# Issuing the modulation's row tiles from GpSimd instead of SyncE in a six-stage transformer stack

## Chip, cores and metric

The kernel runs on one core of one Trainium2 chip. The metric is the device time of one execution in microseconds (us). The core's five engines have one instruction stream each: TensorE (PE, matrix products; its weight loads are shown as PEld), VectorE (DVE), ScalarE (ACT), GpSimd (POOL) and SyncE (SP). An engine works through its stream in order, and an instruction that waits holds back what stands behind it on the same engine. Transfers are issued by an engine's stream and carried out by 16 DMA engines that all issuers share.

## The reference

Four mixer layers (windowed attention, latent attention, mLSTM, windowed attention) act on 256 latent tokens and 256 context tokens of width 1024; then come a stage with three attention branches and a convolutional feed-forward stage, on the latents alone. What the change touches is the modulation of the four layers: for each layer a vector `c` (and another for the context) goes through a SiLU and a 1024 x 3072 matrix, and the three thirds of the result shift, scale and gate the layer.

```python
def modulation(cvec, w_ada, b_ada):
    return jnp.split(jax.nn.silu(cvec) @ w_ada + b_ada, 3, axis=-1)
...
        sh_l, sc_l, gt_l = modulation(c, w_ada, b_ada)
        sh_c, sc_c, gt_c = modulation(c_ctx, w_ada, b_ada)
        h_l = rmsnorm(x_lat, g_pre) * (1.0 + sc_l[:, None, :]) + sh_l[:, None, :]
        h_c = rmsnorm(x_ctx, g_pre) * (1.0 + sc_c) + sh_c
        y_l, y_c = mixer(h_l, h_c, need_ctx=need_ctx)
        x_lat = x_lat + gt_l[:, None, :] * rmsnorm(y_l, g_post)
```

## The kernel before

Activations stay in SBUF, weights are streamed from HBM once. A weight block is cut into parts of 128 x 1024 float32, 512 KB each. `load_part` (line 351) transfers such a part into one of three raw buffers `wr` (`raw`, line 374, issued on SP; from the feed-forward stage on into `wrd`), has ACT round it to a high half `wh` (line 362) and DVE compute the low half `wl` (line 364). A product of two such numbers is three matrix products: lines 384 to 386 (`gemm_a`) or 396 to 399 (`gemm_b`). `turn` (lines 636 to 646) transposes a normalised tile on PE and applies the scale and shift. The PSUM bank tag `tp` has three buffers, shared by all transposes, by `ada_first` and by the row products below.

The modulation of layer 0's shift and scale is made at the start, in four groups (`ada_first`, line 500): four blocks of 512 KB per group go into the buffers `P4` and `Q4` (line 507, on SP) and into products of line 512. Everything else of the modulation is spread over the layers as filler: `ada_steps` (line 530) is a generator that `run` (line 2061) sets up per layer, with block 2 of this layer (the gate) and blocks 0 and 1 of the next layer (scale and shift). A block is eight row tiles `ar` of 128 x 1024 float32, taken in pairs (`NADA = 2`); the pool tag `ar` has two buffers. One step of the generator first traces the product of the pair that was loaded a step before (`ada_product`, line 547, with the matmuls of line 558) and then the two transfers of the next pair. So a pair's transfers wait until the product before has read the two buffers. Layers 0, 1 and 2 have 24 row tiles each, layer 3 has 8: 80 in all. `earn` (line 401) advances the generator whenever enough matmul columns have been traced, and `drain` runs what is left at the end of a layer. `ada_gate` (line 571) and `ada_columns` (line 587) take the finished block out of PSUM; the first needs eight small transfers `br` and writes the gate to DRAM.

Every transfer of the kernel is issued on SP: `dma` (line 411), `bcast` (line 415) and `raw` (line 374). GpSimd has memsets (lines 459, 462, 1026, 1027, 1233, 1393, 1697, 1758, 1880), the scaling of line 1405 in the mLSTM layer, where DVE's line 1406 uses its result and PE transposes it (line 763), and two operations of the GELU (lines 1611 and 1612), in the three-branch stage and the feed-forward stage.

The order of instructions on each engine is not the program's: the framework plans it at build time, with priority to what is earlier in the program among the instructions whose inputs and buffers are free at that point of the plan. On the chip the streams then run in that fixed order, synchronised by semaphores.

The lines of the filler that carry the order:

```python
self.filler = self.ada_steps([(mod, 2)] + ([(nxt, 0), (nxt, 1)] if nxt is not None else []))
self.pace, self.credit = PACE[l], 0
next(self.filler)
```

Of the kernel before, what the change touches and what calls it, by code (L numbers as in the profile page):

```python
# [267 lines left out]
class Net:  # L268
# [258 lines left out]
    def ada_steps(self, blocks):  # L527

        nc, A = self.nc, self.A
        todo = None
        for mod, b in blocks:
            l = mod["l"]
            parts = WEIGHTS[f"l{l}_ada"].off[0 if l == 0 else b]
            src = A[f"w_l{l}_ada"]
            for i in range(0, len(parts), NADA):
                if todo is not None:
                    self.ada_product(*todo)
                rows = []  # L540
                for off, k, kc, n in parts[i:i + NADA]:
                    r = self.far.tile([128, 1024], F32, name=self.nm("ar"), tag="ar", bufs=NADA)
                    self.dma(r, bass.AP(tensor=src.tensor, offset=src.offset + off, ap=[[n, 128], [1, n]]))
                    rows.insert(0, (k, r))
                todo = (mod, b, rows)
                yield True
        self.ada_product(*todo)
        yield True
# [1560 lines left out]
```

## Time and profile before

| quantity | value |
|---|---|
| median of 3 runs | 1439.38 us (1436.44 to 1439.48) |
| the profiled execution | 1436.94 us |
| its span, first to last instruction | 1435.1 us |
| PE busy | 1407.4 us (98%) |
| DVE busy | 1033.9 us (72%) |
| ACT busy | 735.0 us (51%) |
| POOL busy | 47.9 us (3%) |
| moved by DMA | 203.30 MB, mean 142 GB/s |
| mean granted TensorE clock | 0.998 |

Busy time is the time in which an engine has an instruction running; issuing a transfer is not counted as busy. A matmul's end is modelled, so a busy PE is not a PE at its peak. A wait in the views below is idle time of an engine, put down to what ended it. The chain that ended last is followed back from the last instruction, at each step to what released it.

### The profile page before, as it was taken

What the parts mean: (1) busy time and instruction counts of PE and PEld (TensorE: products, weight loads), DVE (VectorE), ACT (ScalarE), POOL (GpSimd) and SP (SyncE); (2) the same over time, 40 slices, a digit from 0 to 9 for tenths busy, and PEclk for the clock granted to TensorE, in tenths of its full rate; (3) what the DMA queues carried; (4) which work ended last, traced back from release to release, by engine and by line L of the source; (5) the groups of instructions that cost most, each with busy time, mean ns of one, the idle gap of its engine ahead of it and who ended that gap; (6) DMA issues with size and microseconds to landing.
All of it is one profiled execution on the core that took longest, in us unless ns stands there. A gap on an engine that the chain in (4) does not pass through costs nothing.

```text
span 1435.1 us, 23818 instructions
## 1 busy us (share of the span) xinstructions
PE 1407.4 (98%) x9083; PEld 1149.1 (80%) x9083; DVE 1033.9 (72%) x2251; ACT 735.0 (51%) x1447; POOL 47.9 (3%) x68
## 2 busy tenths in 40 slices
PE   6999999999999999999999999999999999999998
PEld 4776667788788777777778776768978899899987
DVE  4587885653788576794766768889787887788873
ACT  3455553442466344553634555566575645565552
POOL 0000000000000000010100000000000000022210
PEclk9999999999999999999999999999999999999999
DMA  9541225345521215514252352157424444555563
GB/s 376 207 170 45 74 68 172 122 140 193 177 72 45 88 32 168 206 50 167 92 206 74 116 185 66 61 175 247 165 89 148 162 132 134 194 199 174 170 204 102
DMA packets 63553, 203.30 MB, mean 142 GB/s; under 512 B 10329, under 2 KB 14543, under 8 KB 63439
## 3 DMA queue, kind: packets, MB, share of 16 engines
q1 hardware_dynamic: 63438, 201.79, 41.7%
q8 instruction: 71, 1.16, 0.3%
q14 instruction: 44, 0.35, 0.1%
HBM read 200.65 MB, written 1.11 MB: 141 GB/s over the span
## 4 chain that ended last, share of the span: by engine, by line
PE 85%; DVE 7%; ACT 3%; DMA 3%; issue 2%; POOL 0%; SPq 0%; ACTq 0%; DVEq 0%; POOLq 0%
PE mm L384 11%; PE mm L386 11%; PE mm L385 11%; PE mm L396 8%; PE mm L399 8%; PE mm L397 8%; PE tp L989 3%; PE tp L984 3%; PE tp L558 3%; PE tp L763 2%; PE S L950 2%; PE S L399 1%; PE S L397 1%; PE S L396 1%; PE S L951 1%
## 5 line engine op out<-in xcount | busy, mean ns | idle before, releaser
L364 DVE TENSOR_TENSOR wl<-wr,wh 128x1024 fp32r<-128x1024 f32 (+5 forms) x172 | 202.0, 1181 | 56.0 <-ACT wh L362 54.1
L396 PE MATMUL mm<-th,wh 128*128 128x256 f32 (+1 forms) x712 | 220.4, 310 | 0.6 <-DVE th L771 0.6
L384 PE MATMUL mm<-wh,th 128*128 128x512 f32 (+4 forms) x544 | 215.2, 396 | 4.2 <-DVE th L645 2.1
L399 PE MATMUL mm<-th,wl 128*128 128x256 f32 (+1 forms) x712 | 217.9, 307 | 0.0
L362 ACT ACTIVATE wh<-wr 128x1024 fp32r<-128x1024 f32 (+5 forms) x172 | 175.1, 1027 | 83.3 <-PE mm L397 27.5
L386 PE MATMUL mm<-wh,tl 128*128 128x512 f32 (+4 forms) x552 | 215.4, 391 | 0.1
L397 PE MATMUL mm<-tl,wh 128*128 128x256 f32 (+1 forms) x696 | 213.4, 307 | 0.0
L385 PE MATMUL mm<-wl,th 128*128 128x512 f32 (+4 forms) x544 | 213.0, 392 | 0.0
L396 PEld LDWEIGHTS mm<-th,wh 128*128 128x128 f32 x712 | 135.7, 191 | 10.4 <-issue 4.4
L399 PEld LDWEIGHTS mm<-th,wl 128*128 128x128 f32 x712 | 135.5, 191 | 5.5 <-issue 1.1
L397 PEld LDWEIGHTS mm<-tl,wh 128*128 128x128 f32 x696 | 132.8, 191 | 5.3 <-issue 1.6
L384 PEld LDWEIGHTS mm<-wh,th 128*128 128x128 f32 x544 | 103.1, 190 | 25.6 <-issue 2.8
L386 PEld LDWEIGHTS mm<-wh,tl 128*128 128x128 f32 x552 | 104.4, 189 | 21.4 <-issue 2.2
L385 PEld LDWEIGHTS mm<-wl,th 128*128 128x128 f32 x544 | 103.1, 190 | 18.0 <-issue 0.8
L963 ACT ACTIVATE P<-S,nm 128x512 f32<-128x512 f32 (+1 forms) x96 | 58.5, 613 | 50.7 <-DVE nm L956 42.0
L364 DVE TENSOR_TENSOR wl<-wrd,wh 128x1024 fp32r<-128x1024 f32 x52 | 64.2, 1239 | 22.8 <-ACT wh L362 22.7
L385 PE MATMUL mm<-P,th 128*128 128x512 f32 x176 | 70.7, 402 | 0.0
L362 ACT ACTIVATE wh<-wrd 128x1024 fp32r<-128x1024 f32 x52 | 53.5, 1050 | 22.0 <-PE mm L385 15.7
L955 DVE TENSOR_REDUCE mx<-S 128x1 f32<-128x512 f32 (+1 forms) x80 | 54.0, 685 | 11.4 <-PE S L954 9.3
L384 PE MATMUL mm<-Q,th 128*128 128x512 f32 x144 | 57.5, 400 | 0.0
L386 PE MATMUL mm<-Q,tl 128*128 128x512 f32 x144 | 57.5, 399 | 0.0
L984 PE MATMUL tp<-eye,P 128*128 128x128 f32 x320 | 56.5, 281 | 0.0
(530 smaller groups left out, 3093.4 us busy)
## 6 DMA issues: line engine op xcount, KB each, us to landing
ar<-in_w_l_ada_dram SPq DMA_DIRECT2D x80, 512.0 KB
wr<-in_w_l_in_dram SPq DMA_DIRECT2D x48, 512.0 KB
wr<-in_w_l_out_dram SPq DMA_DIRECT2D x32, 512.0 KB
wr<-in_w_s_mg_dram SPq DMA_DIRECT2D x24, 512.0 KB
wrd<-in_w_s_down_dram SPq DMA_DIRECT2D x22, 512.0 KB
wrd<-in_w_s_gate_dram SPq DMA_DIRECT2D x20, 512.0 KB
wrd<-in_w_s_up_dram SPq DMA_DIRECT2D x20, 512.0 KB
wr<-in_w_s_br_dram SPq DMA_DIRECT2D x12, 512.0 KB
```

Source lines behind the costliest of these rows:

```text
L362: nc.scalar.activation(hi[:, :kc * n], raw[:, :kc * n], AF.Copy)
L364: nc.vector.tensor_sub(lo[:, :kc * n], raw[:, :kc * n], hi[:, :kc * n].bitcast(F32))
L384: nc.tensor.matmul(ps, xh(kk), wh[:, k, n0:n0 + n], start=kk == 0, stop=False)
L385: nc.tensor.matmul(ps, xh(kk), wl[:, k, n0:n0 + n], start=False, stop=False)
L386: nc.tensor.matmul(ps, xl(kk), wh[:, k, n0:n0 + n], start=False, stop=kk == KC - 1)
L396: nc.tensor.matmul(ps, wh[:, k, n0:n0 + m], xh(kk), start=kk == 0, stop=False)
L397: nc.tensor.matmul(ps, wh[:, k, n0:n0 + m], xl(kk), start=False, stop=False)
L399: nc.tensor.matmul(ps, wl[:, k, n0:n0 + m], xh(kk), start=False, stop=kk == KC - 1)
L558: return self.nc.tensor.matmul(ps[32 * g:32 * g + 32, :], self.cs[:, k, :], r[:, g * 256:(g + 1) * 256], start=k0 == 0 and i == 0, stop=k0 ...
L955: nc.vector.reduce_max(mx[:, r0:r0 + per], ps, axis=AX)
L963: nc.scalar.activation(p[:, :nk], ps[:, i, :], AF.Exp, scale=scale, bias=nm[:, r:r + 1], accum_out=sm[:, r:r + 1])
L984: nc.tensor.transpose(tp[:, r, :], P[r][:, j * 128:(j + 1) * 128], self.eye)
```

## The change

The two transfers of a step's row tiles are issued from GpSimd's stream instead of SP's. Source, destination, sizes, buffers and program order are the same, and all other transfers stay on SP.

```diff
@@ -540,7 +540,8 @@
                 rows = []
                 for off, k, kc, n in parts[i:i + NADA]:
                     r = self.far.tile([128, 1024], F32, name=self.nm("ar"), tag="ar", bufs=NADA)
-                    self.dma(r, bass.AP(tensor=src.tensor, offset=src.offset + off, ap=[[n, 128], [1, n]]))
+                    self.nc.gpsimd.dma_start(r, bass.AP(tensor=src.tensor, offset=src.offset + off,
+                                                        ap=[[n, 128], [1, n]]))
                     rows.insert(0, (k, r))
                 todo = (mod, b, rows)
                 yield True
```

## Rows read from the trace of the kernel before

**Rows 1.** The page: busy time by engine, shares of the chain, transfers of `ar`.

```profile
PE 1407.4 (98%) x9083; PEld 1149.1 (80%) x9083; DVE 1033.9 (72%) x2251; ACT 735.0 (51%) x1447; POOL 47.9 (3%) x68
...
PE 85%; DVE 7%; ACT 3%; DMA 3%; issue 2%; POOL 0%; SPq 0%; ACTq 0%; DVEq 0%; POOLq 0%
...
ar<-in_w_l_ada_dram SPq DMA_DIRECT2D x80, 512.0 KB
```

**Rows 2.** Windows of 25 us: length, busy by engine, granted clock, DMA share, GB/s.

```profile
0.00:25.00 25.00, 13.46 (x152) 8.98 (x153) 10.60 (x38) 9.00 (x17) 0.71 (x10) 0.93 0.94 364
...
sum 1425.00, PE 1401.10 PEld 1144.19 DVE 1032.55 ACT 734.97 POOL 47.87; mean PE 24.58 PEld 20.07 DVE 18.11 ACT 12.89 POOL 0.84
```

**Rows 3.** PE's waits, 25 to 1420 us: us in total, times, longest.

```profile
PE mm L384 <- ACT th L835: 1.6, 1, 1.6
PE tp L763 <- DVE P L1406: 1.5, 4, 0.7
...
PE tp L558 <- DMA ar<-in_w_l_ada_dram: 0.7, 1, 0.7
```

**Rows 4.** Windows of 2 us at the start, columns as in rows 2.

```profile
6.00:8.00 2.00, 0.00 (x0) 0.00 (x0) 1.18 (x7) 0.79 (x2) 0.00 (x0) 1.00 1.05 361
...
14.00:16.00 2.00, 0.46 (x5) 0.22 (x3) 1.94 (x8) 2.00 (x4) 0.00 (x0) 1.00 1.04 418
...
24.00:26.00 2.00, 2.00 (x26) 1.39 (x25) 0.55 (x5) 1.05 (x2) 0.00 (x0) 1.00 1.02 397
```

**Rows 5.** The chain that ended last, 0 to 60 us: start us, us, what.

```profile
5.30 6.89 DMA Q<-in_w_l_mod_dram
12.23 1.11 PE tp L512 x16
...
20.96 0.57 PE tp L512 x14
...
49.56 1.00 PE tp L558 x16
```

**Rows 6.** Instructions of the tile `ar`: durations min/median/max, first and last start.

```profile
L411 SPq DMA_DIRECT2D ar<-in_w_l_ada_dram x80: 327/366/1286, 30.5 to 849.9; - x80
```

**Rows 7.** SP's waits over the span: us in total, times, longest.

```profile
SPq L374 <- DVE wl L364: 588.1, 176, 19.6
SPq L411 <- PE tp L558: 176.0, 38, 26.0
```

**Rows 8.** The chain, 440 to 510 us.

```profile
470.84 4.32 DMA wr<-in_w_l_v_dram
```

**Rows 9.** The chain, 212 to 250 us.

```profile
216.08 1.04 PE tp L558 x16
...
218.09 5.54 DMA ar<-in_w_l_ada_dram
...
236.91 1.00 PE tp L558 x16
```

**Rows 10.** Line 1405: durations min/median/max in ns, first and last start.

```profile
L1405 POOL TENSOR_SCALAR P<-P,den x16: 472/690/1501, 608.6 to 721.8; 128x256 f32<-128x256 f32 x8, 128x512 f32<-128x512 f32 x8
```

**Rows 11.** GpSimd's instructions in order of time: start us, us, what.

```profile
1.12 0.11 POOL L1758 MEMSET css<- 128x1 f32 x1
...
633.64 1.79 POOL L1405 TENSOR_SCALAR P<-P,den 128x512 f32<-128x512 f32 x2 [1.97 <-DVE den L1401]
```

**Rows 12.** SP's issues in order of time.

```profile
10.92 0.33 SPq L411 DMA_DIRECT2D Q<-in_w_l_mod_dram  x1
...
30.52 1.59 SPq L411 DMA_DIRECT2D ar<-in_w_l_ada_dram  x2
...
633.25 0.81 SPq L411 DMA_DIRECT2D ar<-in_w_l_ada_dram  x2
```

**Rows 13.** Lines 624 and 364 on DVE, as in rows 10.

```profile
L624 DVE TENSOR_SCALAR xn<-xc,ry x8: 742/748/754, 8.6 to 822.3; 128x1024 f32<-128x1024 f32 x8
...
L364 DVE TENSOR_TENSOR wl<-wrd,wh x52: 1209/1221/2177, 1245.4 to 1418.6; 128x1024 fp32r<-128x1024 f32 x52
```

## Prediction made before the changed kernel was run

> **What bounds the kernel now.** I began with the engine shares and the chain's shares on the page [rows 1]. TensorE (PE) is busy for 1407.4 of 1435.1 us, 98%, and holds 85% of the chain that ended last, so everything the change can give back lies in 27.7 us of idle time. The windows of 25 us say where that is [rows 2]: 25.00 - 13.46 = 11.5 us in the first window; the windows from 25 to 1425 us hold 1401.10 - 13.46 = 1387.6 of 1400 us, so 12.4 us idle; the remaining 3.8 us lie behind 1425 us. Next I asked what PE waited for from 25 to 1420 us [rows 3]. All entries are short, and nearly all end with ACT or DVE; a transfer appears once, as 0.7 us for a row tile `ar`, and a weight tile `wr` never. After the start, then, TensorE does not wait for the issuing of transfers.
>
> The start is different. In the windows of 2 us [rows 4] the transfers run at 361 to 418 GB/s with the DMA engines full, while PE is idle or has gaps; by 24 us PE is full. The chain of waits says the same [rows 5]: a transfer of the modulation block `Q` (6.89 us), its product of line 512 at 12.23 us, and from there mostly compute. Bytes set the first 12 us, TensorE what follows 24 us.
>
> **What leaves SyncE.** 80 issues at a median of 366 ns [rows 6], 29 us of SP's time, and with them the waits for the product of line 558 that gives a pair's two buffers back: 176.0 us in 38 waits [rows 7]. Queued behind them are the weight loads of line 374. But those stood far longer for DVE to free their own buffers (588.1 us in 176 waits, same rows), and PE never waited for one directly. I take 0; the cover is PE's own stream. As the end of the range I take the two waits in rows 3 with a load or a row tile behind them: 1.6 us (`th`, line 835, behind the `wr` load that [rows 8] shows on the chain) and 0.7 us (`ar`), 2.3 us gained. If instead a weight load, now earlier, collides with a row tile, the loss is bounded by one pair's transfer on the chain, 5.54 us [rows 9].
>
> **What comes to GpSimd.** The same 80 issues, with their waits, in the order of its queue. No transfer of this trace is issued there, so the price is bounded: 0.366 us as on SP from below, 1.5 us, the longest instruction of line 1405, from above [rows 10]. I take 0.69 us, the median of that line, the nearest row on the same engine. 80 x 0.69 = 55 us on an engine that is busy for 47.9 us [rows 1]: no bound. At a layer's end a pair's trip (product at 216.08 us, transfer from 218.09 us [rows 9]) becomes longer by up to 2 x (1.5 - 0.37) = 2.3 us. PE has other work then, and its waits for `ar` come to 0.7 us in all [rows 3]; I take 0. With that cover gone, the three trips between the products at 216.08 and 236.91 us [rows 9] would cost 7 us.
>
> **What moves in time.** The order on each engine is planned at build time, and an idle engine gets work far ahead of its place in the program: the memset of line 1758, which belongs to the mixers near the program's end, runs at 1.12 us [rows 11]. SP was never idle so early, and issued the first pair of row tiles at 30.52 us [rows 12], behind everything ahead of it in the program. On GpSimd only memsets are ahead of it, and its buffers are fresh; so it should go out at about 1.2 us. Its 2 x 512 KB = 1.05 MB [rows 1] then share the DMA engines with the chain of rows 5: at about 410 GB/s (rows 4) that is 2.6 us, on the path. Against it: the pair's product, 1.00 us of PE time and first run at 49.56 us [rows 5], can run in an idle stretch. PE idles for 2.00 us in the window at 6 us and for 2.00 - 0.46 = 1.54 us in the one at 14 us [rows 4], so I let two of the four products of layer 0's first block fit: -2.0 us. The second pair's bytes fall behind 8 us, where they delay modulation tiles whose last issue at 10.92 us [rows 12] stands 10 us ahead of the product at 20.96 us [rows 5]; free, and 2.6 us if that cover is gone. Where the bytes leave, at 30 to 36 us, PE is full: 0. The start: +2.6 - 2.0 = +0.6 us, between -2.0 (the transfer hidden) and +5.2 (two pairs exposed, nothing refilled).
>
> **GpSimd's other work.** The memsets of line 1393 and the 16 scalings of line 1405, in the mLSTM layer, now share a queue with the row tiles. In the trace a pair went out at 633.25 us [rows 12], with line 1405 at 633.64 us right behind it [rows 11]. DVE's line 1406 stands behind line 1405, and for that PE already waits 1.5 us in 4 pieces [rows 3]. I count one issue of 0.69 us there as exposed: +0.7 us. A wait rather than an issue ahead of line 1405 is the first rival.
>
> **Sum.** 0 + 0 + 0.6 + 0.7 = +1.3 us. The profiled execution took 1436.94 us (the span of 1435.1 and 1.84 around it), so 1438.2; the median of the runs, 1439.38, lies 2.44 above the profiled one, so I predict 1440.6 us.
>
> One rule of the skill speaks against the change. The trace shows that DVE and GpSimd can hold each other up: line 364 on `wrd`, 1.22 us at the median, took 2.18 us at the longest, and line 1405 goes from 0.47 to 1.5 us [rows 10, 13]. The Trainium skill, "SBUF — State Buffer", section "SBUF: two separate sides", says that the descriptors of a transfer issued by GpSimd are written by GpSimd's cores, that a DVE operation in its fast two-port mode locks them out, and that whoever comes first blocks the other for a whole instruction. The sum above would not change by it, for a row tile has slack; but DVE would be held up too, which is the third rival. No row of a transfer issued by GpSimd is there to test it.
>
> **Rivals.**
> 1. *GpSimd's queue blocks the mLSTM work (slower).* A row tile's issue waits until PE has done the product that frees its buffer; on SP such waits averaged 176.0 / 38 = 4.6 us [rows 7]. It decides where line 1405 stands behind an issue whose product is still to come: two such places cost 9.2 us, 1448.6 us. For it: the coincidence at 633 us [rows 11, 12]. Against it: the planner queues a transfer about when its buffer is free. Chance 0.17.
> 2. *The start pays in full (slower).* Two pairs ahead and no product refilled, for instance because the row tiles' PSUM tile takes one of the three banks of the tag `tp` through the whole start: +5.2 + 0.7, 1445.3 us. For it: the full DMA engines of rows 4. Chance 0.13.
> 3. *DVE is held up (slower).* If each of 80 issues stops DVE for one operation like line 624, 0.75 us [rows 13], that is 60 us, of which DVE's 7% of the chain [rows 1] would count: +4.2 us, 1443.6 us. Against it: such operations are a small part of DVE's. Chance 0.05.
> 4. *Refilled start and a freer SP (faster).* Three products in the gaps and the first transfer hidden, -3.0, and the 2.3 us of the freer queue: 1439.38 - 5.3 = 1434.1 us. Against it: rows 3 name ACT and DVE. Chance 0.13.
> 5. *Nothing moves.* The planner leaves the row tiles where they were and only the issuing engine differs: 1439.4 us. Against it: the memset of rows 11. Chance 0.07.
>
> **How the numbers follow.** My forecast has 0.45, with a range of its own from 1437 to 1443 us. About 0.2%, 2.9 us, is what a measurement of this kernel can tell from no change. Within it: 0.40 of the forecast and rival 5, 0.47. Slower: rivals 1 to 3 and 0.03 of the forecast, 0.38. Faster: rival 4 and 0.02, 0.15. The range from 1434.5 to 1449.0 us takes in rivals 1, 2, 3 and 5 and leaves out most of rival 4.
>
> **What would show it.** Right: 80 issues on GpSimd, the first two near 1 us; line 558 first below 24 us; the product of line 512 that ran at 12.23 us later by 2 to 3 us; PE's idle time from 25 to 1425 us still near 12.4 us. Wrong: PE waiting for line 1406 for more than 5 us (rival 1), a first window of 25 us with over 5 us more idle (rival 2), line 624 well above 0.75 us (rival 3), or an idle time behind 25 us that falls by several us (rival 4). A first issue of `ar` still at 30 us would refute the whole account of the start.

## The result, and the profile after

The changed kernel took **1448.4 us** (median of 6 runs, 1446.5 to 1456.5) beside 1438.8 us for the kernel before (6 runs, 1436.4 to 1439.5): a ratio of 1.0085, 95% interval 1.007 to 1.0099. It is slower by some 10 us; I had forecast +1.3 us. The profiled execution took 1448.34 us with a span of 1446.6 us, 11.5 us above the span of before. (Some line numbers in the part ahead of the prediction are off by one to three: `ada_first` starts at line 499, `earn` at 402, `ada_steps` at 527, `ada_product` at 550, `ada_gate` at 572. In the traces from here on a line behind 543 has moved by one, so line 558 is L559, 1405 is L1406, 624 is L625.)

The page of the changed kernel, engines and the row tiles' transfers, against [rows 1]:

```profile
PE 1411.2 (98%) x9083; PEld 1150.4 (80%) x9083; DVE 1034.4 (72%) x2251; ACT 735.0 (51%) x1447; POOL 92.7 (6%) x148
...
q0 software_dynamic: 11520, 41.95, 8.1%
...
ar<-in_w_l_ada_dram POOLq DMA_DIRECT2D x80, 512.0 KB, 4.4
```

The 80 transfers are GpSimd's now. TensorE's idle time is 1446.6 - 1411.2 = 35.4 us, 7.7 more than before, and it is busy for 3.8 us longer with the same 9083 matmuls. Both have to be explained. Where the idle time is, the windows of 25 us say (columns as in [rows 2]: length, busy time of PE, PEld, DVE, ACT, POOL, granted clock, DMA share, GB/s):

```profile
0.00:25.00 25.00, 11.09 (x111) 7.42 (x115) 9.49 (x36) 8.14 (x15) 2.05 (x12) 0.93 0.93 358
...
50.00:75.00 25.00, 22.37 (x161) 18.04 (x160) 16.39 (x24) 12.74 (x20) 3.16 (x6) 0.86 0.76 245
...
825.00:850.00 25.00, 23.59 (x139) 17.76 (x139) 18.22 (x40) 10.69 (x22) 2.29 (x4) 1.00 0.67 242
```

The first window has 13.9 us of idle time (11.5 before), that from 50 us has 2.6 us (before: none) and a granted clock of 0.86, that from 825 us has 1.4 us, where the kernel before had 0.09:

```profile
825.00:850.00 25.00, 24.91 (x146) 18.93 (x145) 16.16 (x26) 12.39 (x21) 0.00 (x0) 1.00 0.68 225
```

These three make 2.4 + 2.6 + 1.3 = 6.3 of the 7.7 us. What TensorE waited for from 25 to 1420 us, against [rows 3] (us in total, times, longest):

```profile
PE tp L559 <- DMA ar<-in_w_l_ada_dram: 4.4, 4, 2.6
PE tp L764 <- DVE P L1407: 2.0, 4, 0.7
PE mm L384 <- ACT th L836: 1.6, 1, 1.6
```

Of these only the first line has changed much: the row products, which had waited once for 0.7 us, now wait four times. (A wait of 1.2 us for DVE's `K`, line 1122, is new and was not looked into.) In order of time, the second pair's issue (GpSimd), its transfer in the chain of waits, and the products (PE):

```profile
53.15 1.05 POOL L543 DMA_DIRECT2D ar<-in_w_l_ada_dram  x2 [50.34 <-PE tp L559]
```

```profile
53.67 7.07 DMA ar<-in_w_l_ada_dram
```

```profile
60.78 1.94 PE L559 MATMUL tp<-ar,cs 128*32 128x256 f32 x16 [2.63 <-DMA ar<-in_w_l_ada_dram]
```

The pair lands 60.74 - 53.15 = 7.6 us after its issue. The planned order of PE wants it earlier: 60.78 - 2.63 = 58.15 us, 6.0 us behind the start of the first product (52.18 us). In the kernel before the same two products stood 9.3 us apart, with 47 instead of 20 rows of PE's timeline between them, so the order planned at build time has drawn this product forward (why is not shown; the planner's prices were not looked at):

```profile
49.49 1.07 PE L558 MATMUL tp<-ar,cs 128*32 128x256 f32 x16
58.83 1.07 PE L558 MATMUL tp<-ar,cs 128*32 128x256 f32 x16
```

By these numbers the old order would not have waited here: the pair landed 60.74 - 52.18 = 8.6 us behind the start of the first product, and the old order asked for it after 9.3 us. The earlier product and the time of the pair's trip make this stop together.

The second product's sixteen matmuls take 1.94 us instead of 1.07. The windows of 2 us around it show why:

```profile
58.00:60.00 2.00, 0.15 (x2) 0.00 (x0) 1.93 (x7) 0.38 (x1) 0.00 (x0) 1.00 1.04 315
60.00:62.00 2.00, 1.22 (x12) 0.59 (x16) 0.56 (x1) 0.00 (x0) 0.00 (x0) 0.57 1.03 409
62.00:64.00 2.00, 2.00 (x14) 1.35 (x7) 0.00 (x0) 0.00 (x0) 1.06 (x2) 0.50 0.73 233
64.00:66.00 2.00, 2.00 (x11) 2.00 (x11) 0.18 (x1) 0.81 (x3) 0.00 (x0) 0.50 0.95 333
66.00:68.00 2.00, 2.00 (x15) 2.00 (x14) 1.47 (x2) 1.39 (x3) 0.00 (x0) 0.72 0.34 139
68.00:70.00 2.00, 2.00 (x19) 2.00 (x18) 1.75 (x3) 2.00 (x3) 0.00 (x0) 1.00 0.38 74
```

TensorE stands still in the window at 58 us, and behind that its granted clock is 0.50 (the lower level, 1.2 of 2.4 GHz) until some time after 66 us. A clock of 0.86 over the 25 us from 50 is 0.14 x 25 = 3.5 us of work lost. A stop of 2.6 us so costs about 6 us, and the 3.5 us are nearly the whole of the 3.8 us by which PE is busy longer.

### The profile page after: what moved, and what is told of

Read it like the earlier page. It is cut to its first block, busy times and chain, and to the rows that moved or that the text cites. A ratio compares the mean times of both kernels' runs of the same rounds, so it can differ in the third digit from the quotient of the medians.

```text
span 1446.6 us, 23850 instructions
## 1 busy us (share of the span) xinstructions
PE 1411.2 (98%) x9083; PEld 1150.4 (80%) x9083; DVE 1034.4 (72%) x2251; ACT 735.0 (51%) x1447; POOL 92.7 (6%) x148
## 4 chain that ended last, share of the span: by engine, by line
PE 57%; issue 25%; DMA 10%; DVE 5%; ACT 2%; POOL 1%; POOLq 0%; ACTq 0%; DVEq 0%
DMA ar<-in_w_l_ada_dram 9%; PE mm L384 7%; PE mm L386 7%; PE mm L385 7%; PE mm L396 5%; PE mm L399 5%; PE mm L397 5%; PE S L397 1%; PE S L399 1%; PE S L396 1%; PE tp L990 1%; PE tp L764 1%; PE tp L559 1%; PE tp L985 1%; POOL ar L543 1%
## 5 line engine op out<-in xcount | busy, mean ns | idle before, releaser
L543 POOL DMA_DIRECT2D ar<-in_w_l_ada_dram x80 | 43.5, 547 | 761.0 <-PE tp L559 758.9
```

Of the source, the lines that this page charges most:

```text
L543: self.nc.gpsimd.dma_start(r, bass.AP(tensor=src.tensor, offset=src.offset + off, ap=[[n, 128], [1, n]]))
```

## The experiments

**The theory (A).** Transfers issued by GpSimd do not stand in SyncE's line any more; they share the DMA engines with whatever SyncE issues beside them, so they come ahead of bytes that were due first (the start) and behind bytes that were not (the products). **Rivals:** a price on each transfer from GpSimd (B), the new order of TensorE's work in layers 1 to 3 (C), and the two of the prediction that put the loss on GpSimd's queue or on DVE. All experiments on the issuing engine have this edit in `ada_steps`, with another condition each:

```
-  self.nc.gpsimd.dma_start(r, ...)
+  eng = self.nc.gpsimd if CONDITION else self.nc.sync
+  eng.dma_start(r, ...)
```

**1. All but the first pair on GpSimd.** CONDITION: `not (l == 0 and b == 2 and i == 0)`.

> Only the first pair of row tiles goes back to SyncE, the other 78 stay on GpSimd. TensorE's order keeps the second product as early as in the changed kernel. Theory A (the loss is made of the first pair's bytes at the start, 2.4 us, and of TensorE's stop at the second product with the low clock behind it, about 6 us): the first 25 us are as before again, the stop of 2 to 3 us near 58 us stays, about 1446 us. Theory B (a price per transfer that GpSimd issues, 9.6 us / 80 = 0.12 us): 78 of 80 remain, 1448 us. Theory C (the new order in layers 1 to 3): 1448 us.

Measured: 1444.9 us, ratio 1.0053 (1.0036 to 1.007). The first window has 10.4 us of idle time (13.9 after the change), so the first pair is what the start pays for. But A had expected the stop near 58 us to stay, and the waits there are down to 0.5 us with the clock at 1.00; a new stop has appeared at 832 us, of a pair that went out at 821.70 us:

```profile
832.38 1.93 PE L559 MATMUL tp<-ar,cs 128*32 128x256 f32 x16 [4.14 <-DMA ar<-in_w_l_ada_dram]
```

**2. Layer 0's first block on SyncE, the rest on GpSimd.** CONDITION: `not (l == 0 and b == 2)`.

> The four pairs of layer 0's first block go back to SyncE, the other 72 transfers stay on GpSimd; TensorE's order is nearly that of the kernel before. Theory A: start and stop both vanish and only late landings at the ends of layers remain, 1439 to 1441 us. Theory B: 72 x 0.12 = 8.6 us remain, 1447 us. Theory C: as theory A, since the order is the old one; so this run parts A and C from B only.

Measured: 1445.4 us, ratio 1.0049 (1.0032 to 1.0067). (Its runs spread from 1440.7 to 1449.3 us, more than those of the kernel before, 1434.3 to 1440.2 beside them; the profiled one took 1448.4, so its stops are probably among the longer ones.) Theory A as I had put it, with the loss only in layer 0's first 100 us, fails here. B's 1447 us lies within the spread of the runs, but the time is not spread over the transfers: three products wait, near 85 us (1.87 us, and a clock of 0.93 in the 25 us from 75 us), near 227 us (1.30 us) and, longest, near 836 us (4.49 us, 0.86 in the 25 us from 825 us). The windows of 2 us at the longest, PE's lines for the first and the last of the three, the last one's pair in the chain of waits, and the issues of GpSimd and of SP:

```profile
830.00:832.00 2.00, 2.00 (x14) 1.43 (x12) 0.20 (x1) 0.82 (x2) 0.00 (x0) 1.00 1.00 373
832.00:834.00 2.00, 0.04 (x1) 0.00 (x0) 1.61 (x3) 0.69 (x2) 0.00 (x0) 1.00 1.00 404
834.00:836.00 2.00, 0.00 (x0) 0.00 (x0) 0.00 (x0) 0.00 (x0) 0.00 (x0) 0.98 0.46 188
836.00:838.00 2.00, 1.47 (x16) 0.59 (x16) 0.00 (x0) 0.00 (x0) 0.06 (x1) 0.50 0.05 18
```

```profile
84.73 1.74 PE L559 MATMUL tp<-ar,cs 128*32 128x256 f32 x16 [1.87 <-DMA ar<-in_w_l_ada_dram]
...
836.53 1.93 PE L559 MATMUL tp<-ar,cs 128*32 128x256 f32 x16 [4.49 <-DMA ar<-in_w_l_ada_dram]
```

```profile
826.41 10.08 DMA ar<-in_w_l_ada_dram
```

```profile
825.51 1.57 POOL L544 DMA_DIRECT2D ar<-in_w_l_ada_dram  x2 [80.00 <-PE tp L559]
```

```profile
819.70 5.89 SPq L374 DMA_DIRECT2D wr<-in_w_l_in_dram  x4
826.32 0.99 SPq L411 DMA_DIRECT2D xc<-in_w_s_w_dram  x2
```

The pair of 1.05 MB takes 10.08 us, while the last of SP's weight parts of up to 0.5 MB each are in flight or just issued and two more loads (`xc`, the three-branch stage's first weights) follow 0.8 us behind it. What the two queues moved during the trip, from 826.41 to 836.49 us (q1 is SP's queue, q0 GpSimd's; packets, MB, share of the 16 engines):

```profile
q1 hardware_dynamic: 559, 2.03, 53.0%
q0 software_dynamic: 288, 1.05, 27.7%
```

At about 400 GB/s, what the windows show at most, 1.05 MB alone would be an estimated 2.6 us and the 3.08 MB of both queues 7.7 us. The rest is the trip's end: in the window at 834 us the rate is down to 188 GB/s with the DMA engines busy for 0.46 of the time, for a reason that was not looked for. In the kernel before the pair of this place stood in SP's line, ahead of two weight parts and of the `xc` loads, and its product at 827.86 us waited for nothing, with as long from issue to product (6.7 us) as PE's order left in experiment 2 (836.53 - 4.49 - 825.51 = 6.5 us). So here it is the trip that has changed:

```profile
821.13 0.80 SPq L411 DMA_DIRECT2D ar<-in_w_l_ada_dram  x2
822.03 3.56 SPq L374 DMA_DIRECT2D wr<-in_w_l_in_dram  x2
825.64 0.43 SPq L411 DMA_DIRECT2D xc<-in_w_s_w_dram  x1
```

```profile
827.86 1.07 PE L558 MATMUL tp<-ar,cs 128*32 128x256 f32 x16
```

So theory A was widened: **the stop comes wherever a product stands close behind its pair and SP has loads to issue beside it**, in layer 0, at layer ends and in layer 3.

**3. Only layer 0's first block on GpSimd.** CONDITION: `(l == 0 and b == 2)`.

> The reverse: only the four pairs of layer 0's first block on GpSimd, 72 transfers on SyncE, with TensorE's order of the changed kernel. Theory A: start and stop are both there, 1445 to 1448 us. Theory B: 8 x 0.12 = 1 us, 1440 us. Theory C: the order is the new one, 1446 us and more, but without a stop of TensorE near 58 us and a lower clock behind it.

Measured: 1443.9 us, ratio 1.0045 (1.0031 to 1.0058). First window 13.2 us idle, 50 to 75 us 1.8 us, 825 to 850 us 0.2 us, clock 1.00 in all three. That is less than the 1445 to 1448 us of A, more than the 1440 us of B and less than the 1446 us of C: the stop near 58 us, 1.4 us, had no low clock behind it. The eight transfers took 4.7 to 8.2 us to land.

**4. Only the first pair on GpSimd.** CONDITION: `(l == 0 and b == 2 and i == 0)`.

> Only the first pair on GpSimd, 78 transfers on SyncE; TensorE's order is the new one from the third product on, and the second product stands 8 rows later than in the changed kernel, 19 rows earlier than before. Theory A: the start costs its 2.4 us, and the stop at the second product is shorter by the 8 rows and by the quicker issue, 0 to 1.5 us: 1441 to 1444 us. Theory B: 1439 us. Theory C: 1446 us and more, with no loss at the start.

Measured: 1442.7 us, ratio 1.0034 (1.002 to 1.0047): two of 80 transfers cost about 5 us, which rules out B (1439 us) and, with the loss at the start, C (1446 us and more). 13.5 us are idle in the first window, no stop near 58 us, and 1.0 us of waits for `ar` (0.25 and 0.74 us at the end of layer 0).

**5. The start without GpSimd.** The kernel before, everything on SyncE, with the first pair hoisted to the front of its line:

```
+  for off, k, kc, n in WEIGHTS["l0_ada"].off[0][:NADA]:   # ahead of layer 0's first loads
+      r = self.far.tile([128, 1024], F32, ...); self.dma(r, ...); self.hoist.append(r)
...
-  r = self.far.tile(...); self.dma(r, ...)
+  if self.hoist: r = self.hoist.pop(0)
+  else: r = self.far.tile(...); self.dma(r, ...)
```

> No transfer is issued by GpSimd: everything is on SyncE, as before, but the first pair is put at the front of SyncE's stream, ahead of the startup loads (where GpSimd had issued it, in effect). Theory A: the start loses what it lost with GpSimd, since the cause is the 1.05 MB ahead of the loads the start waits for and not the engine that issues them: idle time in the first 25 us 13.5 to 14.1 us instead of 11.5, and 1441 to 1443. A rival by which GpSimd's way of issuing is itself the cause: within 1 us of the kernel before (1438 to 1440), with 11.5 us idle in the first 25 us.

Measured: 1442.8 us, ratio 1.0039 (1.0025 to 1.0053), the time that theory A gave and outside the rival's; the start lost rather more than A gave. The pair goes out on SP at 3.08 us, and the first window has 14.64 us of idle time:

```profile
3.08 0.91 SPq L411 DMA_DIRECT2D ar<-in_w_l_ada_dram  x2
```

```profile
0.00:25.00 25.00, 10.36 (x82) 7.01 (x82) 9.66 (x36) 8.00 (x14) 0.71 (x10) 1.00 0.93 363
```

**The start's loss is the bytes put ahead, not the engine that issues them.** On GpSimd, where they share the DMA engines with the start's loads, it is 2.4 us; in SP's line, ahead of the loads, 3.1 us. A 1.05 MB transfer is an estimated 2.6 us. (The start also varies where nothing in it was changed: 10.4 to 11.0 us idle in experiments 1, 2, 6 and 7, at a clock of 1.00 as here, and 11.5 us at 0.93 in the kernel before. Against the former the loss is 2.2 to 3.1 us in experiments 3 and 4 and 3.6 to 4.2 us in this one.) The rest of this run's 5.4 us stays open (see the end of the next section).

**6. Layer 0's and layer 3's block 2 on SyncE, the other 64 transfers on GpSimd.** CONDITION: `not (b == 2 and l in (0, 3))`.

> Pairs of block 2 of layer 0 and of layer 3 (the ones with nothing but a short wait between pair and product) go back to SyncE; the other 32 pairs stay on GpSimd. Theory A, widened (the loss is made where a pair from GpSimd shares the DMA engines with weight loads that SyncE issues beside it and its product stands close behind it: in the first 25 us, near 58 us, and near 830 us): all three places fall away, small stops near 84 us and at the ends of layers 0 to 2 stay (1 to 3 us with their low clock): 1439 to 1441.5, TensorE's idle time between 825 and 850 us below 0.5 us, in the first 25 us below 11.8 us. Theory B (every transfer issued by GpSimd costs the same): 64 of 80 stay, so 0.8 of 9.6 us: 1446 to 1447.

Measured: 1439.7 us, ratio 1.0024 (1.0014 to 1.0034). The first window's idle time is 11.0 us, no product waits near 58 or 830 us, and the waits for `ar` come to 1.8 us. With 80% of the transfers left on GpSimd, about 70% of the loss is gone.

**7. The stop at 836 us, with the loads that share the DMA engines put behind the pair.** Experiment 2, with the early `xc` and `mg` loads of line 1716 issued by GpSimd too, in one line with the row tiles:

```
 def w1_part(self, w, i, t=None):
+    early = t is not None
...
-    self.dma(t, ...)
+    eng = self.nc.gpsimd if early else self.nc.sync
+    eng.dma_start(t, ...)
```

> As the run with layer 0's pairs of block 2 on SyncE and the rest on GpSimd (1445.4, with a stop of 4.5 us at 836 us), but the four early loads of the convolution's weights into the context's tiles and the merge's buffer are issued by GpSimd too, so that they stand behind the pair of 825 us in one stream instead of beside it. Theory A, widened: the pair lands about 2.6 us earlier (two transfers of 0.52 MB fewer in front of its end), the stop at 836 us falls from 4.5 to about 2 us and the time to 1442 to 1443.5. If the 10 us trip is GpSimd's own, whatever runs beside it: stop 4 us or more, time 1445 to 1446. A pair that waits behind the early loads in GpSimd's stream (the loads wait for the context's tiles) would show as a new stop after 845 us.

Measured: 1440.2 us, ratio 1.0022 (1.0013 to 1.0031), against 1.0049 in experiment 2. The same pair, its two followers, its transfer and its product:

```profile
822.24 1.59 POOL L544 DMA_DIRECT2D ar<-in_w_l_ada_dram  x2 [80.02 <-PE tp L559]
823.82 1.05 POOL L1718 DMA_DIRECT2D xc<-in_w_s_w_dram  x2
```

```profile
816.44 9.97 SPq L374 DMA_DIRECT2D wr<-in_w_l_in_dram  x5
```

```profile
823.16 6.48 DMA ar<-in_w_l_ada_dram
```

```profile
829.68 1.07 PE L559 MATMUL tp<-ar,cs 128*32 128x256 f32 x16 [0.89 <-DMA ar<-in_w_l_ada_dram]
```

```profile
828.00:830.00 2.00, 1.11 (x13) 0.58 (x15) 1.20 (x3) 1.43 (x3) 0.00 (x0) 1.00 1.03 401
830.00:832.00 2.00, 2.00 (x26) 1.46 (x19) 0.62 (x1) 0.58 (x2) 1.05 (x2) 1.00 0.96 391
```

The `xc` loads are still issued at once behind the pair, with the same bytes; the edit has changed only the line they stand in. What the two queues moved during the trip, from 823.16 to 829.64 us:

```profile
q0 software_dynamic: 442, 1.63, 76.3%
q1 hardware_dynamic: 131, 0.47, 20.2%
```

With the pair landed 0.98 MB less than in experiment 2, an estimated 3.1 us at the 305 to 324 GB/s of the two trips. The trip is 6.48 instead of 10.08 us, 3.6 us less, of which I had expected 2.6; the stop is 0.89 instead of 4.49 us, and the clock stays at 1.00, which I had not put into the expected time of 1442 to 1443.5 us. Two things keep this from being a test of the `xc` loads alone: the planner also sent SP's weight parts out earlier, so that about 0.5 MB less of them ran beside the pair, and the stop near 84 us, which the edit does not touch, is 0.76 us at a clock of 1.00 here. SP's weight parts run beside the pair in both kernels, and the trip is still above the 2.6 us of its own bytes.

The Trainium skill, "DMA: Bandwidth & Descriptors", section "Issuing engines are not separate DMA queues", says that transfers of SyncE and of GpSimd run on the same 16 DMA engines and interleave. Experiments 2 and 7 agree: 2.03 MB of SP's queue moved within the pair's 10.08 us, and 0.47 MB within its 6.48 us.

None of the seven beats the kernel before; the nearest, experiments 6 and 7, are 0.2% above it. Four buffers for `ar`, which would let a pair be issued earlier, were not tried.

## Why the prediction was wrong

- **"At a layer's end a pair's trip (...) becomes longer by up to 2 x (1.5 - 0.37) = 2.3 us. PE has other work then, (...) I take 0."** This is the step that failed. It priced the issue, which is cheap (median 0.53 us, below; I took 0.69), and not the place in the line. On SP a pair stood ahead of loads that were issued later; on GpSimd it shares the DMA engines with them. The transfers, 5.54 us in [rows 9], took 7.07 us (58 us) and 10.08 us (experiment 2), while PE's order left 58.15 - 53.15 = 5.0 and 6.5 us from the issue. And the cover was gone not only at a layer's end, where I had looked for it, but near 58 us, where the planner had also drawn the product forward, and in layer 3. The wait itself, 4.4 - 0.7 = 3.7 us, lies within the "7 us if the cover is gone" of that step; behind the longest of them comes the clock with 3.5 us more, which no step had.
- **"If instead a weight load, now earlier, collides with a row tile, the loss is bounded by one pair's transfer on the chain, 5.54 us."** This names the collision that came, but it was neither in the sum nor among the rivals, and the bound was too small: the waits of 3.7 us and the clock's 3.5 us make 7.2 us, and a pair's transfer took up to 10.08 us.
- **"The start: +2.6 - 2.0."** The first half was right: the pair went out at 1.31 us (I said about 1.2), cost 2.4 us, and the products of line 512 moved by 2.7 to 2.8 us (the one at 12.23 us to 14.97 us, within the forecast 2 to 3 us); experiment 5 shows that it is the bytes. The second half failed: no row product was refilled into an idle stretch, the first one ran at 52.18 us (the sign said below 24 us). The second pair's bytes did no harm at the start, for its issue waited for that product.
- **"PE's idle time from 25 to 1425 us still near 12.4 us"** failed as well: it is 17.6 us.
- **"What leaves SyncE: 0"** was right. SP's waits for DVE to free buffers grew from 588.1 us [rows 7] to 788.4 us, 200 us more, as much as the waits (176.0 us) and issues (29 us) that left: the freed time went into them.

```profile
SPq L374 <- DVE wl L364: 788.4, 181, 65.3
```

- **Line 1405, +0.7 us:** DVE's line behind it made PE wait 2.0 us, 0.5 more than in [rows 3]. Right in size.
- **Rival 1** (GpSimd's queue blocks the mLSTM work), whose 1448.6 us is by coincidence the time that came, is false: its mark was over 5 us of waiting for L1406 or the line behind it, and it is 2.0. GpSimd did wait for the products, 758.9 us in 39 waits, with nothing of weight behind it.
- **Rival 2** (the start pays 5.2 us) is false: 2.4 us, with one pair ahead, not two.
- **Rival 3** (DVE is held up) is false: line 624 and line 364 on `wrd` [rows 13] have the medians 748 and 1219 ns (748 and 1221 before), and DVE is busy for 1034.4 us instead of 1033.9.

```profile
L625 DVE TENSOR_SCALAR xn<-xc,ry x8: 743/748/753, 12.0 to 832.5; 128x1024 f32<-128x1024 f32 x8
...
L364 DVE TENSOR_TENSOR wl<-wrd,wh x52: 1214/1219/2184, 1256.8 to 1430.0; 128x1024 fp32r<-128x1024 f32 x52
```

The rule of the Trainium skill, "SBUF — State Buffer", that I set beside it leaves no mark in these rows. Rivals 4 and 5 fell with the sign.

**The account.** Of the profiled difference of 11.5 us: start 2.4, stop near 58 us 2.6 and the low clock behind it 3.5, stop near 839 us 1.3; together 9.8. Of the rest 1.4 us is, on balance, idle time in several windows (0.6 from 225 us, 0.5 from 1225 us among them) and 0.3 us busy time.

**What stays open.** Experiments 3 to 5 have PE busy for 1409 to 1410 us instead of 1407.4, without a low clock in the windows from 50 or 825 us. Nor is it the clock elsewhere: by all windows of 25 us it took 3.5 us in the kernel before (0.93 in those from 0 and 475 us), 1.8 us in experiments 3 and 5 and 3.5 us in experiment 4. The cause is open; their order of PE's work is another one than before, and whether that is it was not tried. Near 58 us no run varies the place of the product and the pair's trip one at a time. And since each change of an issuing engine moves the planner's order too, the size of each stop belongs to the order that came with it: experiments 1 and 4 add up to about the whole (5.3 + 3.4 against 8.5 thousandths), but experiment 1 loses at 832 us what the changed kernel loses at 58.

## What to carry to other kernels

Moving transfers to an idle engine does not only move the issues: it takes them out of the order in which they stood among the others. Ask, for each consumer that follows closely on its transfer, which bytes stood behind it in the old line and would now run beside it; a first estimate of the price is those bytes over the DMA rate, and where it stops a full TensorE, there can be a lower clock for some microseconds behind it. Where the order is planned at build time, look also at whether the consumer has moved closer to its transfer. And a transfer on an engine that is idle at the program's start may be planned to go out at once, as here at 1.31 us: it takes DMA time from the loads that the start waits for.

## What the runs showed of the hardware that I had not expected

An issue on GpSimd is short, and the trip from issue to landing has a wide spread (the changed kernel's tile `ar`, durations min/median/max in ns, then the landing in us):

```profile
L543 POOL DMA_DIRECT2D ar<-in_w_l_ada_dram x80: 527/530/1007, 1.3 to 861.5; - x80
...
DMA to landing us min/median/max: 3.4/4.4/7.5
```

In experiments 1 and 2 the longest trips were 9.7 and 10.1 us with the median still 4.4 us: nothing in a mean tells of them.

TensorE's clock made some stops dearer than their length, and others not: behind 2.63 us (58 us), 4.14 us (experiment 1) and 4.49 us (experiment 2) the rows show 0.50 for about 6 us, behind 1.87 us (experiment 2, near 85 us) for a shorter time, behind 1.17 us (839 us) and 0.89 us (experiment 7) 1.00. Nor does one place always cost the same: in the window from 475 us, where every kernel has 2.4 to 2.9 us of idle time, the clock is 0.93 in the kernel before, 0.86 in experiment 4 and 1.00 in experiment 1:

```profile
475.00:500.00 25.00, 22.34 (x93) 17.60 (x92) 10.42 (x23) 6.30 (x12) 0.00 (x0) 0.93 0.19 60
...
475.00:500.00 25.00, 22.56 (x96) 17.84 (x95) 11.13 (x16) 8.49 (x15) 0.00 (x0) 0.86 0.29 91
...
475.00:500.00 25.00, 22.41 (x102) 17.81 (x101) 11.96 (x23) 6.90 (x13) 0.00 (x0) 1.00 0.21 70
```
